# The output gate as a fifth seven-product pair, with the heads' steps reordered

## The chip, the cores and the metric

The kernel runs on one core of one Trainium2 chip. The metric is the device time in microseconds (us). The core has a matrix engine, TensorE (PE), whose weight loads the profile shows apart (PEld); a vector engine (DVE); a scalar engine (ACT); GpSimd (POOL); and SyncE (SP), which issues most of the transfers. Each engine works through its own instructions in order; semaphores tie them together.

## The reference

One layer of an encoder for 256 tokens of width 2048, in float32. The parts are a SwiGLU feed-forward part (width 5632) with a layer norm, a mixer with a layer norm, a second SwiGLU part with a layer norm, and a gated embedding at the end. The change touches the mixer alone, which computes:

```python
proj = x @ w_in
mq, mk, mv, mo, mi, mf, sq, sk, sv, ga, gb = _split_cols(proj)
qk = silu(_causal_conv(concatenate([mq, mk]), conv_w))
h = _mlstm_chunkwise(q_m, k_m * 256 ** -0.5, mv, log_i, log_f)      # 4 heads of 256
h = _head_norm(h, norm_g)
y_m = h * sigmoid(mo)                                               # mo: the output gate, 1024 columns
y_sb = _stick_breaking(sq, sk, sv)                                  # 8 heads of 128
merged = sigmoid(ga) * (y_m @ w_up_m) + sigmoid(gb) * (y_sb @ w_up_sb)
return merged @ w_out
```

## The kernel before, in words

The tokens stand in two halves of 128 (index `t`). Every large product is a list of **units**. A unit takes 256 rows of a weight (one tile of 128 x 2 x up to 512 columns) and one half of the tokens. Both operands are split into a high and a low float32r part, so that a unit is two k-halves of three matmuls (lines 1210 to 1215). A weight tile is loaded by a transfer on SP's queue (`loads`, line 1128). It is then split: ACT copies out the high part (line 1162), DVE subtracts to give the low one (line 1166). `limits` (line 1116) says how many raw tiles may be loaded ahead and how many splits may stand ready. In the mixer these two numbers are `room`, set on the way by `rooms(...)` entries in the program.

**Seven products for eight.** `seven` (line 321) multiplies the two token halves by two weight blocks with Strassen's scheme: 7 products instead of 8, from sums of weight blocks and from sums of activations (`act.forms`, made by `form_turn`, line 286). The sums of weights are made partly by accumulating transfers on POOL's queue (`grow`, line 337), partly on DVE (`plus`, line 342). The results gather in four PSUM banks named X, E, B, W; B and W are two banks kept for it (`seeded`). `done(m, banks)` is called as each product ends. `chained` (line 374) strings several such pairs together, so that the first product of the next pair runs within the present one, and puts in empty places (`None`) where a sum has to land first. `weave` (line 157) spreads this side list evenly over a main list.

**The order of work.** The Python program itself fixes the order of instructions on every engine. It walks the list of units and keeps a clock of its own, `sched.now`, that each unit pushes on (line 1216). Small steps (transposes, heads, activations) are generators in a heap. Each `yield DELAY[...]` sets a step due so many microseconds later on that clock, and due steps are written out between two units. `wait(...)` asks again every 0.6 us whether a flag is set; `sched.until` runs steps early if a unit needs them. A delay that is too short lets an in-order engine stand before work that is not ready.

**The mixer.** After the first query columns and the gates' columns (line 924) the main list runs: key columns of heads 0 and 1, value columns, output-gate columns `mo`, then queries, keys, values and `mo` of heads 2 and 3, then the six column groups of the stick-breaking heads, then the products with `w_up_m` (`ups(g, 0)`). The side list woven in is the four pairs of merge gates (`gates7`). `mo_done` (line 784) takes each group of `mo` out of PSUM by a sigmoid on ACT and multiplies it with the norm's weights on POOL. `conv` (line 745) transposes and convolves queries and keys. `mlstm(h)` (line 813) is one head: decay matrix (line 817), scores (828), values (840), norm, gate (861), transposes (866). The heads run two in sequence, `mlstm(0)` and `mlstm(1)`, later `mlstm(2)` and `mlstm(3)`. Their outputs are kept in DRAM for a while: `away` (line 798) stores them, `back` (line 804) loads them shortly before they are needed, both on POOL's queue. `stick(h)` (line 875) is one stick-breaking head, two chains of four; it has two masks on POOL (lines 891 and 900) and ends in the matmul of line 906.

All tiles of 4 KB per partition (raw, split, activations, gates) come from one pool of 44 pages; a new tile waits until the last user of its page is done.

Of the kernel before, what the change touches and what calls it, by code (L numbers as in the profile page):

```python
# [8 lines left out]
F32 = mybir.dt.float32  # L9
# [4 lines left out]
P = 128  # L14
# [31 lines left out]
    "sbt": 6.0, "g0": 3.0, "g1": 4.0, "g2": 12.0, "cv0": 1.0, "cv1": 6.0, "turn": 3.5, "apart": 9.0, "copied": 2.5, "away": 6.0, "refill": 14.0, "cv2": 1.3,  # L46
    "m0": 3.0, "m1": 0.6, "m2": 1.2, "m3": 4.6, "m4": 4.6, "s0": 6.6, "s1": 6.7, "s2": 4.0,
# [133 lines left out]
def kernel(  # L181
# [563 lines left out]
    def conv(which, g, stage):  # L745
        yield from wait("cw")
        for e in range(2):
# [8 lines left out]
            acc = temp().rearrange("q (k s) -> q k s", s=S)  # L756
            for k in range(2):
                b = 8 * which + 2 * h + k
                w = lambda j: st["cw"][:, j * 16 + b:j * 16 + b + 1]
                activate(acc[:, k], ps[:, k], ACT.Copy, scale=w(3))  # L760
                for j in range(3):
                    d = 3 - j
                    nc.vector.scalar_tensor_tensor(out=acc[:, k, d:], in0=ps[:, k, :S - d], scalar=w(j),
                                                   in1=acc[:, k, d:], op0=ALU.mult, op1=ALU.add)
# [19 lines left out]
    def mo_done(g):  # L784
        def done(ps, t):
            if ("mo", t) not in st:
                st["mo", t] = big()
            cs = slice(g * COL, (g + 1) * COL)
            activate(st["mo", t][:, cs], ps, ACT.Sigmoid)
            nc.gpsimd.tensor_tensor(out=st["mo", t][:, cs], in0=st["mo", t][:, cs],  # L790
                                    in1=st["nm"][:, cs], op=ALU.mult)
# [21 lines left out]
    def mlstm(h):  # L813
        yield from wait("gates", ("qk", 0, h), ("qk", 1, h), ("v", 0, h // 2), ("v", 1, h // 2))
# [41 lines left out]
        yield from wait(("mo", 0, h // 2), ("mo", 1, h // 2))  # L856
# [396 lines left out]
```

## Time and profile before

| | us |
|---|---|
| median of 3 runs | 2198.45 |
| the three runs | 2197.73, 2198.45, 6001.9 |
| profiled execution | 2197.17 |
| its span, first to last instruction | 2195.5 |
| PE busy | 2175.7 (99%) |
| DVE busy | 1789.3 (82%) |
| ACT busy | 1333.5 (61%) |
| POOL busy | 241.2 (11%) |

The third run took 6001.9 us; the other two lie within 0.03% of each other. A row of a group of instructions in the profile reads: line, engine, operation, what it writes <- what it reads, shapes, count | busy us, mean ns of one | idle time of the engine just before them, and what ended it. A row of waits reads: who <- for whom: us in total, times, longest. A row of a timeline reads: start, duration, engine, line, operation. L with a number is a line of the kernel.

### The profile page before, as it was taken

The numbers are of one execution on the slowest core, as the hardware profiler recorded it, in microseconds if no ns is written. First come the engines' busy times: TensorE is split into PE (matmuls) and PEld (weight loads), VectorE is DVE, ScalarE is ACT, GpSimd is POOL, SyncE is SP. The second block draws the span as 40 slices with busy tenths as digits, with TensorE's granted clock in tenths as the row PEclk, the third lists the DMA queues.
The fourth block names the chain that finished last, engine by engine and source line by source line (L and its number), as shares of the span: only waits on it lengthen the run. The fifth ranks groups of instructions, "written<-read, shape, count | busy, mean of one in ns | idle before, by whom it ended". The sixth has DMA issues, their size and how long they took to land.

```text
span 2195.5 us, 27768 instructions
## 1 busy us (share of the span) xinstructions
PE 2175.7 (99%) x9972; PEld 1801.3 (82%) x9972; DVE 1789.3 (82%) x1967; ACT 1333.5 (61%) x1600; POOL 241.2 (11%) x209
## 2 busy tenths in 40 slices
PE   9999999999999999999999999999999999999999
PEld 7888888888887888888887888888888888888878
DVE  6889988888898778877676777599898989889884
ACT  6556565666575666766575644556666666666562
POOL 3111101111100001011022100011011101110000
PEclk9999999999999999999999999999999999999999
DMA  9899889887993858879678876679878998899652
GB/s 347 221 256 268 254 240 301 270 245 208 292 328 115 255 140 255 225 225 270 206 196 252 261 265 200 213 161 316 262 228 243 305 259 248 241 278 300 214 167 72
DMA packets 274346, 527.06 MB, mean 240 GB/s; under 512 B 16640, under 2 KB 25760, under 8 KB 273952
## 3 DMA queue, kind: packets, MB, share of 16 engines
q1 hardware_dynamic: 229248, 435.10, 58.5%
q0 software_dynamic: 44960, 90.19, 22.4%
q8 instruction: 78, 1.28, 0.2%
q14 instruction: 60, 0.49, 0.1%
HBM read 518.93 MB, written 6.29 MB: 239 GB/s over the span
## 4 chain that ended last, share of the span: by engine, by line
PE 94%; DVE 2%; ACT 2%; issue 1%; DMA 1%; POOL 0%; DVEq 0%; ACTq 0%
PE mm L1214 26%; PE mm L1215 25%; PE mm L1213 25%; PE seeded L1214 5%; PE seeded L1215 5%; PE seeded L1213 5%; PE ms L267 1%; DVE split L1166 1%; ACT split L1162 1%; DMA aside<-actT 1%; ACT temp L239 0%; PE ms L456 0%; POOL temp L891 0%; PE ms L906 0%; PE ms L840 0%
## 5 line engine op out<-in xcount | busy, mean ns | idle before, releaser
L1166 DVE TENSOR_TENSOR split<-raw,split 128x1024 fp32r<-128x1024 f32 (+2 forms) x1061 | 1241.6, 1205 | 221.5 <-ACT split L1162 209.5
L1162 ACT CAST split<-raw 128x1024 fp32r<-128x1024 f32 (+2 forms) x1061 | 1066.8, 1038 | 443.0 <-PE mm L1214 119.1
L1213 PE MATMUL mm<-split,actT 128*128 128x512 f32 (+2 forms) x2640 | 1026.7, 389 | 2.8 <-ACT big L1069 2.3
L1214 PE MATMUL mm<-split,actT 128*128 128x512 f32 (+2 forms) x2640 | 1015.3, 385 | 4.7 <-DVE split L1166 4.7
L1215 PE MATMUL mm<-split,actT 128*128 128x512 f32 (+2 forms) x2640 | 1015.3, 385 | 2.3 <-DVE actT L272 2.3
L1214 PEld LDWEIGHTS mm<-split,actT 128*128 128x128 f32 x2640 | 496.4, 188 | 103.0 <-DVE split L1166 8.3
L1215 PEld LDWEIGHTS mm<-split,actT 128*128 128x128 f32 x2640 | 495.9, 188 | 102.1 <-DVE actT L272 3.1
L1213 PEld LDWEIGHTS mm<-split,actT 128*128 128x128 f32 x2640 | 496.2, 188 | 99.7 <-ACT big L1069 3.2
L337 POOL DMA_DIRECT2D raw<-in_ffn_w_dram x128 | 153.9, 1216 | 1159.8 <-DVE split L1166 961.9
L342 DVE TENSOR_TENSOR raw<-raw 128x1024 f32<-128x1024 f32 x160 | 195.3, 1221 | 12.8 <-DMA raw<-in_ffn_w_dram 10.6
L1214 PE MATMUL seeded<-split,actT 128*128 128x512 f32 x480 | 187.1, 390 | 1.8 <-DVE split L1166 1.8
L1213 PE MATMUL seeded<-split,actT 128*128 128x512 f32 x480 | 188.6, 393 | 0.0
L1215 PE MATMUL seeded<-split,actT 128*128 128x512 f32 x480 | 187.0, 390 | 0.0
L571 DVE SCALAR_TENSOR_TENSOR xres<-mm,xres 128x512 f32<-128x512 f32 x160 | 109.1, 686 | 21.9 <-PE mm L1215 21.9
L1214 PEld LDWEIGHTS seeded<-split,actT 128*128 128x128 f32 x480 | 90.2, 188 | 20.6 <-DVE split L1166 2.5
L1215 PEld LDWEIGHTS seeded<-split,actT 128*128 128x128 f32 x480 | 90.1, 188 | 18.8
L1213 PEld LDWEIGHTS seeded<-split,actT 128*128 128x128 f32 x480 | 90.2, 188 | 18.0
L269 ACT CAST actT<-ms 128x512 fp32r<-128x512 f32 x60 | 35.2, 587 | 85.2 <-PE ms L267 85.1
L337 POOL DMA_DIRECT2D raw<-in_w_in_dram x32 | 38.5, 1208 | 269.8 <-DVE split L1166 262.8
L272 DVE TENSOR_TENSOR actT<-ms,actT 128x512 fp32r<-128x512 f32 x60 | 41.1, 686 | 25.0 <-ACT actT L269 15.2
L239 ACT ACTIVATE temp<-mm 128x512 f32<-128x512 f32 (+1 forms) x38 | 21.8, 574 | 57.8 <-PE mm L1215 57.8
L235 ACT ACT_TABLE_LOAD x36 | 46.2, 1283 | 0.6
(154 smaller groups left out, 724.5 us busy)
## 6 DMA issues: line engine op xcount, KB each, us to landing
raw<-in_ffn_w_dram SPq DMA_DIRECT2D x527, 512.0 KB, 8.0
raw<-in_w_in_dram SPq DMA_DIRECT2D x168, 512.0 KB, 5.0
raw<-in_ffn_w_dram POOLq DMA_DIRECT2D x128, 512.0 KB, 9.4
raw<-in_w_in_dram POOLq DMA_DIRECT2D x32, 512.0 KB, 8.1
raw<-in_w_out_dram SPq DMA_DIRECT2D x32, 512.0 KB, 4.9
raw<-in_w_ple_gate_dram SPq DMA_DIRECT2D x24, 512.0 KB, 5.4
raw<-in_w_up_m_dram SPq DMA_DIRECT2D x16, 512.0 KB, 5.3
raw<-in_w_up_sb_dram SPq DMA_DIRECT2D x16, 512.0 KB, 5.2
```

What stands on the lines that cost most here:

```text
L235: nc.scalar.preload_act_table_set(table[0])
L267: nc.tensor.transpose(ps[:, k], src[:, k * P:(k + 1) * P], ident[:])
L269: nc.scalar.copy(dst[:, 0], ps[:])
L272: nc.vector.tensor_tensor(out=dst[:, 1], in0=ps[:], in1=dst[:, 0], op=ALU.subtract)
L337: nc.gpsimd.dma_start(out=raw.tile[:, :, :cols], in_=src.src, accum_op=ALU.add)
L342: nc.vector.tensor_tensor(out=a.tile[:, :, :cols], in0=a.tile[:, :, :cols], in1=b.tile[:, :, :cols], op=ALU.add)
L571: nc.vector.scalar_tensor_tensor(out=xs, in0=ps, scalar=0.5, in1=xs, op0=ALU.mult, op1=ALU.add)
L1162: nc.scalar.copy(hi[:, ks], r[:, ks])
L1166: nc.vector.tensor_tensor(out=lo[:, ks], in0=r[:, ks], in1=hi[:, ks], op=ALU.subtract)
L1213: nc.tensor.matmul(ps, hi, w[0][:, k, :u.cols], start=first, stop=False, skip_group_check=u.onto)
L1214: nc.tensor.matmul(ps, hi, w[1][:, k, :u.cols], start=False, stop=False, skip_group_check=u.onto)
L1215: nc.tensor.matmul(ps, lo, w[0][:, k, :u.cols], start=False, stop=last, skip_group_check=u.onto)
```

## The change

The output gate leaves the main list. Its two groups of 512 columns become the two weight blocks of one more seven-product pair, put ahead of the four pairs of merge gates in the side list. The code of `gates7` becomes `sigmoid7`, which both use. A sigmoid's result is then multiplied with the norm's weights on DVE, 2.5 us later on the program's clock, and not on POOL. A head now waits for its half of the output gate before its first step and no longer before its last ones; head 2 waits 9 more. Three delays grow (cv0, m1, s2). In `conv` both ACT copies come before the DVE sums. Some `rooms` are smaller, and one stands earlier. `back` comes eight entries before the end of the column groups instead of four, and loads on SP's queue instead of POOL's; the stored tiles are float32 on both sides.

```diff
-    "sbt": 6.0, "g0": 3.0, "g1": 4.0, "g2": 12.0, "cv0": 1.0, "cv1": 6.0, ...
-    "m0": 3.0, "m1": 0.6, "m2": 1.2, "m3": 4.6, "m4": 4.6, "s0": 6.6, "s1": 6.7, "s2": 4.0,
+    "sbt": 6.0, "g0": 3.0, "g1": 4.0, "g2": 12.0, "cv0": 2.5, "cv1": 6.0, ...
+    "m0": 3.0, "m1": 2.5, "m2": 1.2, "m3": 4.6, "m4": 4.6, "s0": 6.6, "s1": 6.7, "s2": 5.5,
...
+            w = lambda k, j: st["cw"][:, j * 16 + 8 * which + 2 * h + k:j * 16 + 8 * which + 2 * h + k + 1]
             for k in range(2):
-                b = 8 * which + 2 * h + k
-                w = lambda j: st["cw"][:, j * 16 + b:j * 16 + b + 1]
-                activate(acc[:, k], ps[:, k], ACT.Copy, scale=w(3))
+                activate(acc[:, k], ps[:, k], ACT.Copy, scale=w(k, 3))
+            for k in range(2):
                 for j in range(3):
...
-    def mo_done(g):
-        def done(ps, t):
...
-            activate(st["mo", t][:, cs], ps, ACT.Sigmoid)
-            nc.gpsimd.tensor_tensor(out=st["mo", t][:, cs], in0=st["mo", t][:, cs],
-                                    in1=st["nm"][:, cs], op=ALU.mult)
-            flags.add(("mo", t, g))
-        return done
+    def mo_place(t, g):
+        if ("mo", t) not in st:
+            st["mo", t] = big()
+        return st["mo", t][:, g * COL:(g + 1) * COL]
+
+    def mo_after(t, g):
+        c = mo_place(t, g)
+        sched.spawn(mo_scaled(t, g, c), DELAY["copied"])
+
+    def mo_scaled(t, g, c):
+        nc.vector.tensor_tensor(out=c, in0=c, in1=st["nm"][:, g * COL:(g + 1) * COL], op=ALU.mult)
+        flags.add(("mo", t, g))
...
-    aside = {(c, t): dram_pool.tile([P, 2, 4, P], F32R, name=f"aside{c}{t}") for c in range(2) for t in range(TT)}
+    aside = {(c, t): dram_pool.tile([P, 2, 4, P], F32, name=f"aside{c}{t}") for c in range(2) for t in range(TT)}
...
-        nc.gpsimd.dma_start(out=aside[c, t][:], in_=ymT.tiles[c, t][:])
+        nc.gpsimd.dma_start(out=aside[c, t][:], in_=ymT.tiles[c, t][:].bitcast(F32))
...
-                nc.gpsimd.dma_start(out=ymT.tiles[c, t][:], in_=aside[c, t][:])
+                nc.sync.dma_start(out=ymT.tiles[c, t][:].bitcast(F32), in_=aside[c, t][:])
...
     def mlstm(h):
-        yield from wait("gates", ("qk", 0, h), ("qk", 1, h), ("v", 0, h // 2), ("v", 1, h // 2))
+        yield from wait("gates", ("qk", 0, h), ("qk", 1, h), ("v", 0, h // 2), ("v", 1, h // 2),
+                        ("mo", 0, h // 2), ("mo", 1, h // 2))
+        if h == 2:
+            yield DELAY["apart"]
...
-        yield from wait(("mo", 0, h // 2), ("mo", 1, h // 2))
...
-            main += [rooms(9)] + columns(COL, COL, qk_done(0, 1)) + [rooms(9)] + columns(1024 + COL, COL, qk_done(1, 1))
+            main += [rooms(9)] + columns(COL, COL, qk_done(0, 1)) + [rooms(8)] + columns(1024 + COL, COL, qk_done(1, 1))
...
-        main += columns(3072 + g * COL, COL, mo_done(g))
...
-            main.append(rooms(12 if first == 2 else 10))
+            main.insert(len(main) - (0 if first == 2 else 6), rooms(11 if first == 2 else 7))
...
-    def gates7(g):
+    def sigmoid7(wa, wb, col0, place, after):
...
-        def gate(t, half, src, sign):
+        def part(t, half, src, sign):
             activate(place(t, half), src, ACT.Sigmoid, scale=sign)
-            flags.add(("gate", g, half, t))
+            after(t, half)
...
+        return seven(wa, wb, D, col0, COL, x1T, done)
...
-    main.insert(len(main) - 4, back)
+    main[len(main) - 8:len(main) - 8] = [back]
...
-    program.extend(weave(main, chained([gates7(g) for g in range(4)])))
+    program.extend(weave(main, chained([sigmoid7(w_in[:, 3072:], w_in[:, 3072 + COL:], 0, mo_place, mo_after)] + [gates7(g) for g in range(4)])))
```

More of the change, by code (lines that the diff above doesn't have):

```diff
@@ L782, in load_norm_m @@
         nc.sync.dma_start(out=st["nm"][:], in_=norm_m[0].partition_broadcast(P))
[L784 to L793 removed]
+    def mo_place(t, g):
[8 more added lines that the diff above has]
+        flags.add(("mo", t, g))
+        return
+        yield
     ymT, ysbT = ActT(act_tile), ActT(act_tile)
[L796 removed]
+    aside = {(c, t): dram_pool.tile([P, 2, 4, P], F32, name=f"aside{c}{t}") for c in range(2) for t in range(TT)}
     def away(c, t):
[L799 removed]
+        nc.gpsimd.dma_start(out=aside[c, t][:], in_=ymT.tiles[c, t][:].bitcast(F32))
         pages[0] -= 1
@@ L946 @@
     gt = {}
-    def gates7(g):
-        def place(t, half):
-            if (g, t) not in gt:
-                assert g > 1 or "spilt" in flags
-                gt[g, t] = xres[t][:, g * 1024:(g + 1) * 1024] if g < 2 else big()[:]
-            return gt[g, t][:, half * COL:(half + 1) * COL]
+    def sigmoid7(wa, wb, col0, place, after):
         def done(m, banks):
@@ L968, in done @@
             elif m == 2:
-                sched.spawn(gate(0, 0, ps["X"], 1.0), DELAY["silu"])
+                sched.spawn(part(0, 0, ps["X"], 1.0), DELAY["silu"])
             elif m == 7:
```

19 lines of the change are left out of this document (13 added, 6 removed).

## The prediction

> **What bounds the kernel now.** I read the page from the top: the span, the busy shares, the chain that ended last.
>
> ```profile
> span 2195.5 us, 27768 instructions
> PE 2175.7 (99%) x9972; PEld 1801.3 (82%) x9972; DVE 1789.3 (82%) x1967; ACT 1333.5 (61%) x1600; POOL 241.2 (11%) x209
> PE 94%; DVE 2%; ACT 2%; issue 1%; DMA 1%; POOL 0%; DVEq 0%; ACTq 0%
> ```
>
> TensorE (PE) is idle for 2195.5 − 2175.7 = 19.8 us in the whole run, and 94% of the chain lies on it. The page counts pipelined matmuls as busy, so I check at what pace they come, in the timeline of PE at a place without a gap:
>
> ```profile
> 902.54 0.39 PE L1213 MATMUL mm<-split,actT 128*128 128x512 f32 x1
> ...
> 907.98 0.39 PE L1213 MATMUL mm<-split,actT 128*128 128x512 f32 x1
> ```
>
> Between these rows lie 24 matmuls of 512 columns: 5.44 us, 0.227 us from start to start, although each row lasts 0.39. One work unit of the program (two k-halves of three matmuls) is thus 1.36 us. The time can fall in two ways: fewer matmuls, or less idle PE.
>
> The edits lie in the mixer. I compare windows: mixer, and the second FFN, in which seven-product pairs are woven in more densely.
>
> ```profile
> core 0: us, PE busy (x) PEld busy (x) DVE busy (x) ACT busy (x) POOL busy (x), PEclk, DMA share, GB/s
> 715.00:1260.00 545.00, 539.81 (x2523) 446.37 (x2522) 404.25 (x500) 351.60 (x461) 71.62 (x64) 1.00 0.80 229
> 1420.00:2080.00 660.00, 659.47 (x2955) 545.50 (x2955) 589.89 (x607) 403.56 (x436) 77.24 (x64) 1.00 0.88 257
> ```
>
> In the mixer PE idles 545.00 − 539.81 = 5.19 us at full clock; in the FFN only 0.53 us, with VectorE (DVE) 89% busy against 74% here. So a denser DVE does not by itself cost PE time. The waits of PE in the mixer's window:
>
> ```profile
> PE seeded L1214 <- DVE split L1166: 1.8, 2, 1.2
> PE ms L677 <- DVE big L683: 1.4, 1, 1.4
> PE ms L906 <- POOL temp L900: 0.9, 1, 0.9
> PE mm L1214 <- DVE split L1166: 0.8, 2, 0.7
> PE ms L840 <- DVE temp L830: 0.2, 1, 0.2
> ```
>
> Five causes, 5.1 us together (total, times, longest). That is all that reordering alone can win in this stage.
>
> **The change part by part.** *The matmuls.* Two groups of 512 output-gate columns now take 2 x 8 row pairs x 2 token halves = 32 units. As a seven-product pair they take 7 products x 4 = 28. Four units less is 24 matmuls, on the engine that sets the end: −5.44 us, the very stretch quoted above. The shape, the operands and the banks (mm and seeded) are those of the four pairs already there, so I see no reason for another pace. The Trainium skill (TensorE: Matmul & The Clock Gate, Back-to-back issue gap) gives a sustained spacing of about 131 ns for 512 columns; by it the estimate would be 24 x 0.131 = 3.1 us. The trace disagrees, with 227 ns over 24 matmuls, and decides.
>
> *What the other engines get.* Sixteen weight tiles, each used twice, become 28, each used once: 12 more splits. Besides come 8 sums on DVE (line 342), 8 accumulating loads on GpSimd's (POOL's) queue (line 337), and the copies and differences of the bank work. The products with the norm (line 790) go from POOL to DVE.
>
> ```profile
> L1166 DVE TENSOR_TENSOR split<-raw,split 128x1024 fp32r<-128x1024 f32 x230 | 274.1, 1224 | 94.6 <-ACT split L1162 93.7 <-PE mm L1214 0.2
> L1162 ACT CAST split<-raw 128x1024 fp32r<-128x1024 f32 x230 | 231.6, 1049 | 44.1 <-PE mm L1214 13.5 <-DMA aside<-actT 8.4 <-PE seeded L1214 6.4
> L342 DVE TENSOR_TENSOR raw<-raw 128x1024 f32<-128x1024 f32 x32 | 39.2, 1224 | 2.2 <-DMA raw<-in_w_in_dram 2.2
> L337 POOL DMA_DIRECT2D raw<-in_w_in_dram x32 | 38.5, 1208 | 269.8 <-DVE split L1166 262.8 <-DVE hrs L857 7.0
> L962 DVE TENSOR_TENSOR seeded<-mm,temp 128x512 f32<-128x512 f32 x4 | 2.8, 697 | 2.1 <-ACT temp L960 2.1
> L960 ACT COPY temp<-mm 128x512 f32<-128x512 f32 x4 | 2.3, 585 | 3.4 <-PE mm L1215 3.4
> L790 POOL TENSOR_TENSOR big<-big 128x512 f32<-128x512 f32 x4 | 5.5, 1386 | 35.2 <-ACT big L239 35.1
> L235 ACT ACT_TABLE_LOAD x26 | 33.4, 1283 | 0.5
> ```
>
> DVE: 12 x 1.224 + 8 x 1.224 + about 6 x 0.697 (two in the bank work, four products) = 28.7 us, so 433 us of some 540, 80%. ScalarE (ACT): 12 x 1.049 + 3 x 0.585 = 14.3 us, so 68%; the sigmoids at other times may bring or spare some table loads of 1.283. POOL: 8 x 1.208 − 5.5 = +4.2 us. I cost all of it at nothing: its cover is the splits that stand ready (up to four in the mixer), and the FFN window carries 89% DVE under an idle PE of 0.53 us. Where the cover is gone, a late split costs up to 1.2 us (row of waits).
>
> *Order in time.* Weaving 163 side entries over 200 main units instead of 132 over 232 raises the density from 0.57 to 0.82. To place events I count units of 1.36 us from the start of the weave:
>
> ```profile
> L695 ACT COPY gst<-mm x2: 166/177/188, 743.3 to 743.7; 128x8 f32<-128x8 f32 x2
> 798.95 0.69 PE L817 MATMUL ms<-big 4*128 4x256 f32 x2
> 841.01 0.69 PE L817 MATMUL ms<-big 4*128 4x256 f32 x2
> ```
>
> It starts near 743. The gate's last product is side entry 43, behind 53 main and 32 side units: 743 + 85 x 1.36 = 859, with transposes between some 864. A head waits for it at its front now, so heads 0 and 1 start near 865 and not at 799. A head takes 841.01 − 798.95 = 42.1 us, 44 with the longer m1: the pair runs to 953. The second value columns are done after 131 units, near 935, so head 2 (9 later) overlaps head 1 by some 10 us. This wait is one of the program's writer, not of an engine: nothing is queued behind it. The rest of the stage needs the heads only in the ups, by the same count some 200 us on. The overlap can cost a late split, 0 to 1.2 us twice; I take +0.6.
>
> *Delays.* m1 from 0.6 to 2.5 covers the 0.2 us at line 840. The conv's two ACT copies now stand ahead of its six DVE sums; what it saves, the ACT's idle time between, isn't on PE's path: nothing. cv0 only moves transposes. s2 from 4.0 to 5.5 and the move of `back` act on the 0.9 us at line 906. Its cause:
>
> ```profile
> 1185.80 5.87 POOL L891 TENSOR_SCALAR_AFFINE_SELECT temp<-temp 128x256 f32<-128x256 f32 x1 [3.57 <-DVE temp L890]
> 1191.63 0.40 POOL L900 TENSOR_SCALAR_AFFINE_SELECT temp<-temp 128x256 f32<-128x256 f32 x1
> 1185.64 1.22 DVE L342 TENSOR_TENSOR raw<-raw 128x1024 f32<-128x1024 f32 x1
> 1186.78 4.63 DVE L1166 TENSOR_TENSOR split<-raw,split 128x1024 fp32r<-128x1024 f32 x4
> ```
>
> A mask of 0.4 us took 5.87, and the next one, for which PE waited, stood behind it. 1.5 us more covers 0.9: −0.9 us.
>
> *`back` on SP.* Four loads leave POOL's queue for SP's and come four entries of the main list sooner. On SP the weight loads stand behind them, and ACT's splits wait for those. The nearest rows:
>
> ```profile
> ACT split L1162 <- DMA aside<-actT: 8.4, 2, 7.2
> raw<-in_w_in_dram SPq DMA_DIRECT2D x168, 512.0 KB, 5.0
> actT<-aside POOLq DMA_DIRECT2D x4, 512.0 KB, 8.1
> ```
>
> ACT once stood 7.2 us for a page that an outgoing store still held, and PE lost under 0.8 us by it (the row of waits at mm L1214). Nor does ACT's row of splits name a weight load among its three largest waits, so the smaller rooms (8, 11 and 7 tiles ahead) have slack. Bounds: 0 to 7.2 us; I take 0, near to what PE lost. The ups have no wait for these loads now, so sooner wins nothing.
>
> *Sum.* −5.44 + 0.6 − 0.2 − 0.9 = −5.9 us. The profiled execution took 2197.17 us (span 2195.5), so 2191.2. The timed runs lie higher: 2197.73 and 2198.45 are 0.9 above it on average, and the third, 6001.9, says nothing of the kernel. Forecast: 2192.1 us.
>
> **The rivals.** *All of the mixer's idle time goes* (17%): the delays and rooms act on each of the five causes, so 2198.1 − 5.44 − 5.19 = 2187.4. Against it: 2.6 us of the five are late splits, and splits come more often now.
>
> *The masks hold PE up* (8%, slower than before). Each of eight sticks has a mask just ahead of its last matmul (line 906). If each costs PE the 0.9 us of the one row, that is 6.3 more than now: 2198.1 − 5.44 + 6.3 = 2199.0; at 1.4, the longest wait of the stage, 2203. It decides from the seventh such wait on. For it: the mask of 5.87 us beside five DVE instructions, of which there will be more. Against it: one wait in eight now, and 1.5 us more room. The Trainium skill (SBUF — State Buffer, Who interferes with whom) says that "A DVE instruction with two SBUF inputs contends with a GpSimd instruction that reads SBUF" and that the later one blocks until the first ends; the mask above, which ended 0.26 us after the five, agrees, and by that rule the 24 such instructions added make this rival likelier.
>
> *The loads run dry* (9%): `back` or a store holds SP or a page while few tiles stand ahead, and the 7.2 us of ACT reach PE: 2198.1 − 5.44 + 7.2 = 2199.9, from one occurrence on. Against it: it happened once, and the splits in hand took it.
>
> That the change doesn't do what it says can be left out: 28 units stand in the code.
>
> **How the numbers follow.** The forecast has 62%; its own range, with splits' waits between none and four more of 1.2, is 2189 to 2196. Four per cent remain for what no row shows. The range of 2187 to 2199 takes in the forecast and most of the first rival, and reaches to the lower edge of the other two. Left out are some 5% below 2187, the upper halves of the two slower rivals (9%) and the remainder (4%). Two per cent, about what a measurement of this kernel can tell from no change, are 44 us. Faster by that would need more than all idle PE time (19.8) and the matmuls together: 1%. Slower needs 50 us of new waits, where the longest of PE in the mixer is 1.4, or a second run like 6001.9: 3%. Within: 96%.
>
> **What would show it.** PE's matmuls in the mixer's window fall by 24 at the same 0.227 us. The wait at line 906 is gone, POOL's products too; splits grow by 12, sums by 8. Heads start near 865. PE's waits in the mixer sum to 3 to 7 us. I am wrong if they pass 10, if the masks lead them, if ACT waits for weight loads, or if idle time appears outside the mixer.

## The result and the profile after

The changed kernel took 2218.92 us (median of four runs, 2216.64 to 2221.86), the kernel before 2198.09 (median of the three runs already shown and one more, 2196.72). It is slower by 1%, or 20.8 us, where 6 us less was forecast. The ratio on record, 1.0099 with a 95% interval of 1.0086 to 1.0112, leaves the run of 6001.9 us out, which the medians do not; 20.8 us lies within its interval.

The profiled execution was the slowest of the four, 2221.86 us. The head of its page, the line of the engines and that of the chain's shares:

```profile
span 2220.1 us, 27824 instructions
PE 2182.7 (98%) x9948; PEld 1801.6 (81%) x9948; DVE 1812.8 (82%) x1993; ACT 1348.9 (61%) x1617; POOL 248.2 (11%) x209
PE 85%; DVE 4%; issue 4%; DMA 4%; ACT 3%; POOL 1%; SPq 0%; DVEq 0%; POOLq 0%; ACTq 0%
```

The 24 matmuls are gone (9972 to 9948), yet PE is *busy* 7 us longer, and idle for 37.4 us instead of 19.8. Both belong to the loss: more waiting, and stretches in which matmuls are slower. The windows say where. Columns: window, its length, then busy us and count of PE, PEld, DVE, ACT and POOL, the granted clock of PE (1.00 is full speed), DMA share, GB/s. The first two rows answer to those shown of before:

```profile
715.00:1260.00 545.00, 522.86 (x2398) 427.46 (x2397) 407.28 (x506) 354.18 (x464) 78.15 (x64) 0.98 0.80 226
1420.00:2080.00 660.00, 658.52 (x2952) 544.86 (x2951) 586.66 (x598) 415.42 (x456) 77.30 (x64) 1.00 0.89 259
870.00:930.00 60.00, 50.01 (x208) 39.79 (x208) 43.09 (x64) 35.61 (x46) 4.44 (x4) 0.89 0.50 136
913.00:922.30 9.30, 9.07 (x21) 6.44 (x22) 3.20 (x5) 5.12 (x7) 0.41 (x1) 0.50 0.31 81
```

The mixer's window holds 2398 of PE's instructions, before 2523. Twenty-four no longer exist, so the program is 101 behind at 1260 us, at 0.227 us each 22.9 us: nearly all of the 24.6 by which the span grew. The FFN's window is as full as it was (2952 to 2955). The worst 60 us of the mixer are 870 to 930: 208 instructions at a mean clock of 0.89. Before it held:

```profile
870.00:930.00 60.00, 58.77 (x269) 48.28 (x268) 47.91 (x59) 41.84 (x53) 6.02 (x6) 1.00 0.85 236
```

DVE and ACT did not take PE's place there: they too are less busy than before. The engines stood for each other. PE's waits in the mixer after the change (who <- for whom: us, times, longest; lines 1213 to 1215 are now 1223 to 1225, the split's 1166 is 1176, the product with the values, 840, is 847, the head's transposes 866 are 872):

```profile
PE mm L1224 <- DVE split L1176: 7.3, 8, 1.8
PE ms L872 <- DVE temp L763: 6.9, 1, 6.9
PE ms L847 <- DVE temp L837: 3.3, 1, 3.3
PE mm L1223 <- ACT temp L671: 1.8, 1, 1.8
PE seeded L1224 <- DVE split L1176: 1.5, 4, 0.6
PE ms L901 <- POOL temp L897: 0.2, 1, 0.2
```

With one of 0.5 and one of 0.4 that are left out here they sum to 21.9 us, where before had 5.1. The longest, 6.9 us, is one event. PE's timeline around it (start, duration, line; in brackets the idle time and what ended it):

```profile
895.71 0.39 PE L1225 MATMUL seeded<-split,actT 128*128 128x512 f32 x1
...
900.70 0.39 PE L1223 MATMUL mm<-split,actT 128*128 128x512 f32 x1
902.84 0.50 PE L1224 MATMUL mm<-split,actT 128*128 128x512 f32 x1 [1.76 <-DVE split L1176]
...
905.51 0.60 PE L752 MATMUL ms<-ident,temp 128*128 128x128 f32 x4
905.95 0.38 PE L872 MATMUL ms<-ident,temp 128*128 128x128 f32 x2
913.23 0.66 PE L872 MATMUL ms<-ident,temp 128*128 128x128 f32 x2 [6.90 <-DVE temp L763]
...
918.12 0.63 PE L1224 MATMUL mm<-split,actT 128*128 128x512 f32 x1
...
922.39 0.44 PE L1225 MATMUL mm<-split,actT 128*128 128x512 f32 x1
```

Up to 900.70 the pace is the old one (22 matmuls in 4.99 us, 0.227 each). Then PE transposes a block of keys for the convolution (L752), and at once, with no unit between, head 0's output (L872). The first half of the head's transposes goes through, the second waits until the convolution's sums have been read out of PSUM by DVE. What DVE had ahead of that:

```profile
905.61 1.22 DVE L1176 TENSOR_TENSOR split<-raw,split 128x1024 fp32r<-128x1024 f32 x1
906.75 1.22 DVE L342 TENSOR_TENSOR raw<-raw 128x1024 f32<-128x1024 f32 x1
907.88 2.35 DVE L1176 TENSOR_TENSOR split<-raw,split 128x1024 fp32r<-128x1024 f32 x2
910.15 2.93 DVE L763 SCALAR_TENSOR_TENSOR temp<-ms,cw,temp 128x253 f32<-128x253 f32 x6
```

Between the transposes at 905.5 and the sums at 910.15 stand splits and weight sums: DVE's in-order queue is some 5 us long. The head's own input was ready (its last product, L867, began at 905.27), so what is missing is a PSUM bank; by the code, the two accumulators, X, E, the convolution's block and the head's first half hold all that are left beside B and W. Afterwards the clock is at half for 9.3 us (the row 913.00:922.30): from 918.12 to 922.39 ten matmuls start, one every 0.427 us. The clock had fallen inside the wait: the trace's granted clock changes to a half at 908.82, 2.5 us after the wait began, and back to full at 922.48. Nothing in the prediction had allowed for it. The Trainium skill (TensorE: Matmul & The Clock Gate, What's actually happening, and Wait — 56ns, not 53.3ns?) has the array at half clock after an idle window of about 3.4 us, and a start-to-start of 426.7 ns for 512 columns while cold. The spacing agrees; the idle time does not, for here 2.5 us were enough.

ACT, before, named no weight load among the main causes of its waits. Now:

```profile
ACT split L1172 <- DVE raw L342: 20.3, 12, 3.3
ACT split L1172 <- DMA raw<-in_w_in_dram: 14.4, 5, 6.3
```

One of these, at 966 us, stands ahead of the 3.3 us of line 847. ACT's timeline there:

```profile
966.00 1.05 ACT L1172 CAST split<-raw 128x1024 fp32r<-128x1024 f32 x1 [6.26 <-DMA raw<-in_w_in_dram]
967.07 1.28 ACT L235 ACT_TABLE_LOAD   x1
968.36 0.73 ACT L239 ACTIVATE temp<-ms,aT 128x256 f32<-128x256 f32 x2
```

ACT stands 6.26 us in front of a split whose tile is not there; a head's exponentials (L239, behind a table load) come after it in ACT's order, and the step on PE which needs them is late. Another 2.08 us on the way go to DVE, which waits for the load of a sum until 970.38, and 3.4 to that sum and two splits in front of the head's step.

### The profile page after: what moved, and what is told of

Same layout as the page of the kernel before. It is cut to its first block, busy times and chain, and to the rows that moved or that the text cites. A ratio compares the mean times of both kernels' runs of the same rounds, so it can differ in the third digit from the quotient of the medians.

```text
span 2220.1 us, 27824 instructions
## 1 busy us (share of the span) xinstructions
PE 2182.7 (98%) x9948; PEld 1801.6 (81%) x9948; DVE 1812.8 (82%) x1993; ACT 1348.9 (61%) x1617; POOL 248.2 (11%) x209
## 4 chain that ended last, share of the span: by engine, by line
PE 85%; DVE 4%; issue 4%; DMA 4%; ACT 3%; POOL 1%; SPq 0%; DVEq 0%; POOLq 0%; ACTq 0%
PE mm L1224 23%; PE mm L1225 23%; PE mm L1223 23%; PE seeded L1225 4%; PE seeded L1223 4%; PE seeded L1224 4%; DVE split L1176 2%; DMA raw<-in_ffn_w_dram 2%; ACT split L1172 1%; DMA raw<-in_w_in_dram 1%; PE ms L267 1%; ACT temp L239 1%; DMA aside<-actT 0%; DVE temp L763 0%; PE ms L456 0%
## 5 line engine op out<-in xcount | busy, mean ns | idle before, releaser
L1176 DVE TENSOR_TENSOR split<-raw,split 128x1024 fp32r<-128x1024 f32 (+2 forms) x1073 | 1256.8, 1206 | 214.1 <-ACT split L1172 195.5
L1172 ACT CAST split<-raw 128x1024 fp32r<-128x1024 f32 (+2 forms) x1073 | 1079.6, 1038 | 474.9 <-PE mm L1224 120.2
L1224 PE MATMUL mm<-split,actT 128*128 128x512 f32 (+2 forms) x2608 | 1006.9, 386 | 11.4 <-DVE split L1176 11.3
L1224 PEld LDWEIGHTS mm<-split,actT 128*128 128x128 f32 x2608 | 491.9, 189 | 111.5 <-DVE split L1176 18.1
L342 DVE TENSOR_TENSOR raw<-raw 128x1024 f32<-128x1024 f32 x168 | 204.8, 1219 | 20.2 <-DMA raw<-in_ffn_w_dram 10.4
L1224 PE MATMUL seeded<-split,actT 128*128 128x512 f32 x504 | 197.7, 392 | 1.5 <-DVE split L1176 1.5
L1223 PE MATMUL seeded<-split,actT 128*128 128x512 f32 x504 | 199.1, 395 | 0.0
L1225 PE MATMUL seeded<-split,actT 128*128 128x512 f32 x504 | 197.0, 391 | 0.0
L571 DVE SCALAR_TENSOR_TENSOR xres<-mm,xres 128x512 f32<-128x512 f32 x160 | 109.0, 686 | 21.9 <-PE mm L1225 21.9
L1224 PEld LDWEIGHTS seeded<-split,actT 128*128 128x128 f32 x504 | 95.0, 188 | 22.7 <-DVE split L1176 3.7
L1225 PEld LDWEIGHTS seeded<-split,actT 128*128 128x128 f32 x504 | 95.0, 188 | 19.7
L1223 PEld LDWEIGHTS seeded<-split,actT 128*128 128x128 f32 x504 | 95.2, 189 | 19.4 <-issue 0.3
L337 POOL DMA_DIRECT2D raw<-in_w_in_dram x40 | 48.4, 1215 | 299.3 <-DVE split L1176 216.8
L239 ACT ACTIVATE temp<-mm 128x512 f32<-128x512 f32 (+1 forms) x38 | 21.8, 574 | 58.0 <-PE mm L1225 57.9
```

What stands on the lines that cost most here:

```text
L239: nc.scalar.activation(out, in_, func, **kw)
L337: nc.gpsimd.dma_start(out=raw.tile[:, :, :cols], in_=src.src, accum_op=ALU.add)
L342: nc.vector.tensor_tensor(out=a.tile[:, :, :cols], in0=a.tile[:, :, :cols], in1=b.tile[:, :, :cols], op=ALU.add)
L571: nc.vector.scalar_tensor_tensor(out=xs, in0=ps, scalar=0.5, in1=xs, op0=ALU.mult, op1=ALU.add)
L1172: nc.scalar.copy(hi[:, ks], r[:, ks])
L1176: nc.vector.tensor_tensor(out=lo[:, ks], in0=r[:, ks], in1=hi[:, ks], op=ALU.subtract)
```

## The experiments

Two families of causes were at stake: places (a step that stands badly, a wait that can be moved) and work (more on DVE and in the loads than the mixer can hide). For all of them the table gives the time over the kernel before of the same set of runs (2196.7 to 2197.1 us), and the ratio with its interval; the changed kernel, timed in the first set alone, is 20.8 over. An interval reaches some 1.5 parts in a thousand to each side, about 3 us: smaller differences between two rows are not clear of noise.

| label | us | over before | ratio |
|---|---|---|---|
| pair_alone | 2227.10 | +30.0 | 1.0137 [1.0121, 1.0152] |
| heads_early | 2210.54 | +13.5 | 1.0062 [1.0047, 1.0077] |
| rooms_as_before | 2215.24 | +18.2 | 1.0085 [1.0070, 1.0100] |
| head0_turns_late | 2208.76 | +11.7 | 1.0052 [1.0035, 1.0068] |
| rooms_and_late | 2205.88 | +9.1 | 1.0038 [1.0024, 1.0051] |
| patient | 2206.26 | +9.5 | 1.0043 [1.0027, 1.0060] |
| patient_rooms | 2208.73 | +11.9 | 1.0055 [1.0037, 1.0073] |
| patient_rooms_loads | 2212.29 | +15.5 | 1.0071 [1.0053, 1.0089] |
| splits_five | 2204.91 | +8.2 | 1.0038 [1.0025, 1.0051] |
| splits_six | 2223.00 | +26.1 | 1.0120 [1.0105, 1.0135] |
| raws_more | 2222.20 | +25.5 | 1.0115 [1.0099, 1.0130] |
| sums_ahead | 2210.68 | +14.0 | 1.0061 [1.0046, 1.0076] |
| sums_by_load | 2210.47 | +13.6 | 1.0061 [1.0044, 1.0078] |
| sums_by_load_2 | 2208.44 | +11.7 | 1.0053 [1.0038, 1.0068] |
| all_sums_by_load | 2231.59 | +34.8 | 1.0158 [1.0143, 1.0174] |
| before_more_dve | 2207.93 | +11.1 | 1.0049 [1.0034, 1.0064] |
| before_denser | 2217.99 | +21.3 | 1.0098 [1.0083, 1.0113] |
| pause | 2217.00 | +20.1 | 1.0091 [1.0076, 1.0106] |

Five of them came out above every range that was given for them: `splits_six`, `raws_more`, `all_sums_by_load`, `before_denser` and `patient_rooms`. `heads_early` and `head0_turns_late` lie between the ranges of the two theories.

### The parts of the change

**pair_alone**: the kernel before with the fifth pair and nothing else of the change (the product with the norm on POOL, heads, delays, rooms and `back` as before).

```diff
-        main += columns(3072 + g * COL, COL, mo_done(g))
...
-    program.extend(weave(main, chained([gates7(g) for g in range(4)])))
+    program.extend(weave(main, chained([sigmoid7(w_in[:, 3072:], w_in[:, 3072 + COL:], 0, mo_place, mo_after)] + [gates7(g) for g in range(4)])))
```

> The kernel before with the seven-product pair for the output gate alone: the heads wait for the gate late as before, conv order, delays, rooms and the way back are those of before, the product with the norm stays on POOL. Theory collision (the heads, moved onto the convolutions by their wait at the front, fill VectorE and PSUM; PE waits and its clock then drops): head 0 starts near 800 but is held at its late wait until the gate is done near 864, so part of the collision stays; 2195 to 2208. Theory work (the pair's own splits, sums and loads are too much for the mixer): 2212 or more. Theory rooms (fewer tiles ahead leave ACT waiting for weight loads): 2192 to 2195, no wait of PE over 2 us.

The pair alone costs 30.0 us; the other edits win 9 of it back. PE's waits in its mixer:

```profile
PE mm L1215 <- DMA actT<-aside: 6.4, 1, 6.4
PE mm L1216 <- DVE split L1168: 5.6, 8, 1.8
PE ms L864 <- DVE temp L762: 4.6, 1, 4.6
PE ms L904 <- POOL temp L898: 1.7, 1, 1.7
```

The heads' outputs come back too late by 6.4 us; a mask (L898) holds PE 1.7 us; the changed kernel, with the moved `back` and the longer s2, has neither wait. The head's transposes wait behind the convolution here too (4.6). So the small edits together do their work, though no run takes one of these two out by itself. What they mend is made by the pair.

**heads_early**: the changed kernel, with the heads' wait for the output gate back before the norm, and no 9 us more for head 2.

```diff
-        yield from wait("gates", ("qk", 0, h), ("qk", 1, h), ("v", 0, h // 2), ("v", 1, h // 2),
-                        ("mo", 0, h // 2), ("mo", 1, h // 2))
-        if h == 2:
-            yield DELAY["apart"]
+        yield from wait("gates", ("qk", 0, h), ("qk", 1, h), ("v", 0, h // 2), ("v", 1, h // 2))
...
+        yield from wait(("mo", 0, h // 2), ("mo", 1, h // 2))
```

> The changed kernel, but the heads wait for the output gate only before their norm, as before, and head 2 isn't held back by 9. Theory collision: heads 0 and 1 no longer stand at the same program point as the convolutions' second half; the wait of 6.9 us at the head's transposes and the slow clock behind it go, some 12 to 15 us: 2204 to 2207. Theory work and theory rooms: the heads' place matters little, 2214 or more.

**head0_turns_late**: the changed kernel, with head 0's transposes 9 us later and no other edit.

```diff
-        yield DELAY["m4"]
+        yield DELAY["m4"] + (9.0 if h == 0 else 0.0)
```

> The changed kernel with one delay more: head 0's transposes come 9 us later, seven units behind the convolution's transposes and not right after them. Theory collision: the 6.9 us at the head's transposes was a wait for a PSUM bank that the convolution still held; it goes, with the slow clock behind it: 2204 to 2208. Theories work and rooms: VectorE's backlog is there all the same, PE waits elsewhere for late splits, 2214 or more.

Both take the head off the convolution, and both win: 20.8 over before becomes 13.5 and 11.7. The second is the sharper test, for it moves only head 0's transposes and what follows them in the heads' own order. The line of 6.9 us is gone; late splits remain (11.0 us in 15 waits).

**rooms_as_before**: the changed kernel with the old `rooms`.

```diff
-            main += [rooms(9)] + columns(COL, COL, qk_done(0, 1)) + [rooms(8)] + ...
+            main += [rooms(9)] + columns(COL, COL, qk_done(0, 1)) + [rooms(9)] + ...
...
-            main.insert(len(main) - (0 if first == 2 else 6), rooms(11 if first == 2 else 7))
+            main.append(rooms(12 if first == 2 else 10))
```

> The changed kernel with the rooms of before (9, 12 and 10 tiles ahead instead of 8, 11 and 7). Theory rooms: ACT's waits for weight loads (14.4 us in the mixer) go, and with them the wait of 3.3 us at the values' product and the slow clock behind it: 2208 to 2211, and 2195 if this is all of it. Theory collision: the wait of 6.9 us stays; 2210 to 2219. Theory work: no change, 2216 to 2222.

It wins 2.6 us, less than the intervals can tell by themselves. ACT's waits for weight loads fall from 14.4 to 4.0 us, but PE's 6.9 and the wait at line 847 (3.1) stay. The place of ACT's long wait shows why:

```profile
961.70 1.05 ACT L1172 CAST split<-raw 128x1024 fp32r<-128x1024 f32 x1 [5.42 <-DMA aside<-actT]
```

In front of the same table load and exponentials ACT now stands 5.42 us for a page that the outgoing store of a head still holds. The cause changed, the wait stayed.

**rooms_and_late**: both edits together.

> The changed kernel with head 0's transposes 9 us later and the rooms of before. If the two causes are separate, their gains add: 2218.9 - 10.1 - 3.7 = 2205. If both are one and the same backlog, less than half of the second is left: 2207 to 2209.

9.1 us over before: the two gains add (20.8 − 9.1 − 2.6), and the rooms bring the same 2.6 a second time. PE's waits are then almost of one kind:

```profile
PE mm L1224 <- DVE split L1176: 8.3, 10, 1.8
PE seeded L1224 <- DVE split L1176: 0.8, 1, 0.8
```

With the 5.4 us that the pair saves, some 14.5 us are still lost; in the profiled execution, a faster one of 2204.03 us, 12.2. Waits are only a part of these: PE is idle for 27.4 us (before: 19.8), 7.6 more, and busy for 2174.9, which is 4.6 more than 2175.7 less the 5.4. The clock is full throughout there. Matmuls behind a wait come slower for a while even so (in the changed kernel, after the 1.76 us at 902.84, ten starts take 2.44 us, 0.244 each); no run takes the two parts apart. The rest of the runs asked what the loss is for.

### Is it DVE's added work?

**before_more_dve**: the kernel before, with 24 more operations on DVE where the output gate's weights pass, 29 us of work, and nothing else. Like the sums, they stand between a tile's load and ACT's copy of it (ACT waits 6.6 us for them). They take the maximum of a raw weight tile with itself, in place, so nothing changes in the result.

```diff
+    def extra(raw, n):
+        def make():
+            for _ in range(n):
+                nc.vector.tensor_tensor(out=raw.tile[:], in0=raw.tile[:], in1=raw.tile[:], op=ALU.max)
+        return make
...
-        main += columns(3072 + g * COL, COL, mo_done(g))
+        mo = columns(3072 + g * COL, COL, mo_done(g))
+        for k, u in enumerate(mo[::2]):
+            u.tile.make = extra(u.tile.raw, 1 + k % 2)
+        main += mo
```

> The kernel before with 24 more VectorE instructions of the sums' size at the output gate's weight tiles (each writes the larger of a tile and itself, so nothing is changed by it): 29 us more of VectorE work in the mixer, about what the pair brings, without any other edit. Theory work: 2205 or more. Theory collision: 2197 to 2200, since heads, convolutions and gate stand apart there.

It costs 11.1 us. First the windows' row of its mixer, then PE's waits there:

```profile
715.00:1260.00 545.00, 533.03 (x2477) 439.67 (x2476) 420.21 (x513) 346.06 (x456) 73.00 (x64) 0.99 0.79 225
```

```profile
PE mm L1223 <- DVE split L1175: 2.8, 3, 1.2
PE ms L846 <- DVE temp L836: 2.7, 1, 2.7
PE seeded L1223 <- DVE split L1175: 1.8, 2, 1.2
```

DVE is at 77% (420.21 of 545), far from full. PE's waits rise from 5.1 to 12.0 us: those for splits on DVE from 2.6 to 4.6, all others from 2.5 to 7.4. The longest is at a head's product with the values, which comes before its input is ready now that DVE has more in front of it. The shape of the loss is that of `rooms_and_late`: PE is idle 6.8 us more and busy 3.9 more. This is the run that decides on the term that the prediction put at nothing.

**sums_by_load**, **sums_by_load_2**: `head0_turns_late`, with the new pair's sums of weights made by accumulating loads and not on DVE (8 sums of 1.22 us). In the first a quarter of the output gate is taken before its last product is in, so there its share is missing; the second takes it behind that product.

```diff
-        return seven(wa, wb, D, col0, COL, x1T, done)
+        return seven(wa, wb, D, col0, COL, x1T, done, grown)
...
-    ... 0, mo_place, mo_after)] + [gates7(g) for g in range(4)])))
+    ... 0, mo_place, mo_after, True)] + [gates7(g) for g in range(4)])))
```

> The changed kernel with head 0's transposes 9 us later and, besides, the gate pair's 8 sums on VectorE replaced by accumulating transfers (the scheme's other form, with its third product before the seventh). Theory sums (ACT and so the splits wait behind the pair's sums on VectorE, 22 us of ACT's idle time): half of the waits before 990 us go, 2202 to 2205. Theory elsewhere: 2207 to 2211, or more if the transfers come late.

> As sums_by_load, but the second half's sigmoid of the gate is taken as the seventh product ends and no longer as the third does (there it came a product too early, so that part of the output gate was wrong, and PE waited 6.8 us for it). Theory sums (VectorE's extra work makes splits late): that wait goes and the waits for splits stay low, 2202 to 2204. Theory elsewhere: 2207 to 2211.

No gain (+11.7 both with and without). PE's late splits fall from 11.0 to 6.0 us, but a new wait of 2.6 at a high part comes, and ACT's waits for weight loads rise from 11.3 to 21.0.

**all_sums_by_load**: `rooms_and_late`, with all five pairs' sums made by loads.

> The changed kernel with head 0's transposes 9 us later, the rooms of before, and in all five pairs the sums made by accumulating transfers, none by VectorE: some 49 us less VectorE work in the mixer, 20 transfers more. Theory work (about 0.37 us of time for each us of VectorE work, as before_more_dve showed): 10 us or more below rooms_and_late, 2190 to 2197. Theory transfers: they come late, and what VectorE gives PE loses again, 2200 to 2212.

34.8 us over before. The windows' row of its mixer, then its ACT's main wait there:

```profile
715.00:1260.00 545.00, 520.18 (x2382) 422.37 (x2380) 363.34 (x462) 353.73 (x462) 115.39 (x103) 0.99 0.93 242
```

```profile
ACT split L1175 <- DMA raw<-in_w_in_dram: 44.6, 15, 7.9
```

Over the whole run DVE is busy 41 us less than in `rooms_and_late` (1771.0 for 1812.3). But in the mixer the DMA engines are 93% busy (82% there), and what ACT waits for most is weight loads. Less work on DVE is no help if the transfers pay for it.

### Is it the chain from load to sum to split?

ACT's largest wait in the changed kernel is for sums on DVE (20.3 us). **sums_ahead**: `rooms_and_late`, with each sum in the mixer written one split earlier.

```diff
+                if limits(j) is room:
+                    make(j + 3)
```

> rooms_and_late (2205.9 us as measured) with the sums on VectorE written out one split earlier in the mixer. ACT's 20 us of waiting for sums (14 times) is the mark of a chain: the sum stands behind a subtraction on VectorE, ACT's copy waits for the sum, the next subtraction waits for ACT. Theory chain: with the sum one place ahead ACT's waits fall to 8 us and PE's waits for splits from 8 to 4 us; 2199 to 2202. Theories four splits, loads and density: 2204 to 2208; more if the sums now wait for loads.

**splits_five**, **splits_six**: up to five (six) splits ready instead of four; the first on `rooms_and_late`, the second on `head0_turns_late`.

```diff
-    main = [rooms(13, 4)] + columns(1024, COL, qk_done(1, 0)) + [rooms(8)]
+    main = [rooms(13, 5)] + columns(1024, COL, qk_done(1, 0)) + [rooms(8)]
```

> rooms_and_late with five splits in hand in the mixer instead of four. Theory four splits: PE's waits for splits halve and its waits at the heads' steps, which stand behind more splits, grow less than that; 2200 to 2204. If the lesson of splits_six holds (what the splits gain, the steps of heads and convolutions lose): 2205 to 2212.

> The changed kernel with head 0's transposes 9 us later (2208.8 us as measured) and, besides, six splits in hand in the mixer instead of four. Theory late splits (what is left of the loss, some 13 us against the sum of the prediction, is PE waiting for splits that VectorE finishes late, because each split is now used up in one unit more often than in two): with 7 to 8 us of splits in hand instead of 5 to 6 the waits for splits fall from 11 us to 3; 2198 to 2202. Theory backlog (VectorE itself is too full there): the same waits come later, 2206 to 2210.

**raws_more**: `rooms_and_late` with one or two raw tiles more throughout (14, 10, 11, 11, 14, 12, 12 for 13, 8, 9, 9, 12, 10, 10).

> rooms_and_late with two more raw tiles ahead everywhere in the weave (10, 11, 14 and 12). Theory loads: 2201 to 2203. Else 2204 to 2208, since ACT waits for no weight load there any more.

Each does what it says and none wins. With `sums_ahead` ACT no longer waits for sums, but DVE waits longer for the sums' loads (14.7 us for 6.1), and the time rises by 4.9. With five splits PE's waits for splits fall from 9.1 to some 3 us and those at steps rise by about as much: the time is the same. With six it is 14.4 us worse than its base; of its PE waits:

```profile
PE ms L824 <- DVE actT L262: 5.8, 2, 5.1
PE ms L847 <- DVE temp L837: 5.2, 4, 1.7
PE ms L752 <- ACT temp L740: 4.6, 2, 2.9
PE mm L1224 <- DVE split L1176: 2.5, 3, 1.5
```

The splits are in time now, the steps are late: a split made ahead stands in DVE's and ACT's queues in front of a step that is due. More raw tiles take pages from the 44: ACT's longest waits are then for a page's last readers, DVE (31.1 us) and PE (28.5 us; 13.6 and 15.3 in `rooms_and_late`), and the time rises by 16.4.

### Is it the delays?

**patient**: `head0_turns_late` with longer delays for every step of heads, convolutions and sticks. **patient_rooms**: the same with the old rooms. **patient_rooms_loads**: that with the new pair's sums by loads.

```diff
-    "sbt": 6.0, ... "cv0": 2.5, ...
-    "m0": 3.0, "m1": 2.5, "m2": 1.2, "m3": 4.6, "m4": 4.6, "s0": 6.6, "s1": 6.7, "s2": 5.5,
+    "sbt": 8.0, ... "cv0": 4.5, ...
+    "m0": 5.0, "m1": 4.5, "m2": 1.2, "m3": 7.0, "m4": 8.0, "s0": 8.0, "s1": 8.0, "s2": 7.0,
```

> The changed kernel with head 0's transposes 9 us later and longer delays between the steps of heads, sticks and convolutions (m0 5, m1 4.5, m3 7, m4 8, sbt 8, s0 8, s1 8, s2 7, cv0 4.5); nobody needs these steps early. Theory steps too tight (a fuller VectorE finishes the steps' work later than their delays allow): PE's waits at steps go, but they are only some 5 us of the 16 left: 2203 to 2206. Theory late splits: the splits' waits of 11 us stay, 2206 to 2210.

> Head 0's transposes 9 later, the rooms as before the change, and every step of heads, conv and sticks due 0.8 to 3.4 us later. If the three gains add (2218.9 - 10.2 - 3.7 - 2.5), 2202.5: steps' waits gone, ACT without a wait for weight loads, late splits of 6 to 9 us left. If what is taken from one wait only appears in another: 2205 to 2207, the splits' waits at 9 or more.

> As patient_rooms, and the new pair's sums of weights made by accumulating loads instead of by DVE (8 sums of 1.22 us, 10 us of DVE's work). If DVE's work in the mixer is what makes splits late, their waits fall from some 8 to 4 us and the time to 2198 to 2200. If the loads only take over (as they did with the smaller rooms): the same within 2 us of patient_rooms, with ACT's waits for weight loads back.

With the changed kernel's rooms the longer delays win 2.2 us and the waits at steps go. With the old rooms they lose 2.8 against `rooms_and_late`, though each edit alone was a gain; the intervals overlap in both comparisons. PE's waits for splits are 10.0 us there, those at steps below 2. The sums by loads cost 3.6 more, as ACT's waits for weight loads come back (12.8 us). From here on the gains of single edits no longer add.

### Is it the order alone?

**before_denser**: the kernel before, same work, only that its four pairs are woven over the first 162 main units instead of all; density 0.81, about that of the changed kernel.

```diff
-    program.extend(weave(main, chained([gates7(g) for g in range(4)])))
+    cut = [i for i, u in enumerate(main) if isinstance(u, Unit)][162]
+    program.extend(weave(main[:cut], chained([gates7(g) for g in range(4)])) + main[cut:])
```

> The kernel before with its four pairs woven over the first 162 units of the main list and not over all 232: the density of side entries is 0.81 as in the changed kernel, without any added work. Theory density: waits for splits of 5 to 8 us more, 2201 to 2206. Else 2196 to 2199.

It costs 21.3 us without a single added operation. Its PE waits, in the mixer up to 1300 us, since the stage ends later here:

```profile
PE ms L906 <- POOL temp L900: 4.9, 2, 3.2
PE ms L866 <- DVE actT L262: 4.5, 1, 4.5
PE mm L1215 <- DVE split L1167: 4.1, 5, 1.3
PE ms L895 <- POOL temp L891: 2.3, 1, 2.3
PE ms L752 <- ACT temp L740: 1.4, 1, 1.4
```

The most, 7.2 us, goes to masks of the last sticks (lines 906 and 895). From 1256.35 to 1270.16 PE runs only small matmuls of these sticks, for the next products need their output and no unit stands between, and the clock is at half from 1263.59 to 1273.83. The changed kernel has no such end. Again a head's transposes wait once for long (4.5). Late splits, which the expectation was about, grow little (4.4 us with the `seeded` ones, before 2.6). Delays and rooms of this kernel fit one order of the work; another order pays for that, whether it brings work or not. It isn't the same order as the changed kernel's (here the pairs end early, and no side entries are left for the sticks), so this can't be set against the 14.5 us one to one.

### What does a pause cost beyond itself?

**pause**: the kernel before, with one transpose on PE, after the mixer, that waits for eight operations on POOL.

```diff
...
+        for _ in range(8):
+            nc.gpsimd.tensor_scalar(out=t[:], in0=t[:], scalar1=ALPHA, scalar2=None, op0=ALU.mult)
+        ps = misc([P, P])
+        nc.tensor.transpose(ps[:], t[:, 0:P], ident[:])
...
```

> The kernel before with one pause of PE in the stage of the output weights: one transpose waits for eight GpSimd instructions of about 1.56 us on a tile that nothing else uses, 6 to 10 us of idle PE. Theory clock: behind the pause some 30 matmuls run at half the pace (0.43 us instead of 0.227), so the time grows by the wait plus 5 to 7 us. Theory no clock: it grows by the wait alone, as if the slow stretch in the changed kernel were the backlog's.

```profile
PE ms L1034 <- POOL temp L1032: 16.6, 1, 16.6
```

The span of the profiled execution grew by 18.1 us for a wait of 16.6. The windows' row behind the pause reads:

```profile
1344.30:1348.30 4.00, 4.00 (x12) 3.13 (x12) 0.00 (x0) 0.00 (x0) 0.00 (x0) 0.56 0.00 0
```

Behind the wait half clock lasts 4 us and costs some 1.8 (nine starts of matmuls take 3.86 us; at 0.227 they would take 2.04), less than the expectation had. In the changed kernel the slow stretch behind the shorter wait of 6.9 us lasted 9.3 us. The trace's granted clock says more, if one reads when it changes. It is at half throughout these two windows, of the changed kernel and of `pause`:

```profile
908.90:922.40 13.50, 9.17 (x22) 6.45 (x23) 7.16 (x12) 5.22 (x7) 0.41 (x1) 0.50 0.22 59
1330.80:1347.80 17.00, 3.77 (x10) 3.00 (x11) 8.65 (x6) 2.09 (x2) 12.59 (x8) 0.50 0.31 94
```

The first stretch lasts from 908.82 to 922.48, the second from 1330.78 to 1347.85: 13.65 and 17.07 us, four and five times 3.41. Leaving out the first and last 15 us of each trace, the 20 traces have 33 stretches of half clock, and all are one to five times 3.41 us long. So what a wait costs beyond itself depends on more than its length: the same wait of 6.9 us in `rooms_as_before` began a stretch of 10.24. Why the step from 915.65 to 919.06 in the changed kernel, full of work on PE, did not bring the clock back isn't settled; a head's small matmul (line 824) lies in it.

## Why the prediction was wrong

**The matmuls: right.** 24 fewer, pace 0.227 where nothing waits. The 24 matmuls, 5.44 us at this pace, are gone from the trace; the saving is only smaller than what came with it. Two of the prediction's own signs of being wrong came: waits in the mixer over 10 us (21.9), and ACT waiting for weight loads (14.4).

**"I cost all of it at nothing": the first wrong step.** The counts were right (splits 1061 to 1073 in the whole run, sums 160 to 168), but the cover was chosen by busy share. The FFN window at 89% DVE is another case: 496 of its 590 us are splits and sums, and the program lets five splits and 16 raw tiles stand ready there, against four and 7 to 13 in the mixer. In the mixer DVE, at 74%, also has steps on which PE waits directly, and these stand in order behind the splits. 29 us of work put into the kernel before cost 11.1 us (`before_more_dve`), at 77%. The stated bound, "a late split costs up to 1.2 us", was also low: a late split cost up to 1.8 in the changed kernel, and a late step 2.7 in `before_more_dve` and 3.3 at line 847.

**"The overlap can cost a late split ... I take +0.6": the second.** Head 0 did start where the count put it (line 824 at 869.4; 865 was forecast). The overlap that was priced never came: head 1 ended at 951.5, and head 2 began at 961.3, not near 944. I looked at the overlap of heads with each other and not at what else lies at the heads' new place. Head 0's transposes fell on a block of the convolution of later keys; together they lacked a PSUM bank. `head0_turns_late` shows 9.1 us for it, of which 6.9 are the wait; that the rest is the half clock is read from the trace, not tested by itself.

**"The smaller rooms (8, 11 and 7 tiles ahead) have slack": wrong by some 2.6 us** (`rooms_as_before`). The rival *the loads run dry* had the mechanism, and its price of 7.2 was too high: with the smaller rooms ACT stood 6.26 us for a load, with the old ones 5.42 for a page that a store held, and PE waited 3.3 and 3.1 behind it.

**`back` on SP and the delays: half right.** On SP the loads harmed nothing visible, so 0 of 0 to 7.2 us was right. "Sooner wins nothing" was not: with the pair, the old place and the old queue PE waits 6.4 us for them (`pair_alone`). The wait for the mask at line 906 (now 912) is gone as forecast; 0.2 us are left at the other mask's (901). So the rival *the masks hold PE up* is refuted for this kernel; `pair_alone`, with the old s2, has 1.7 us of it. The 0.2 us at line 840 became 3.3 at 847 instead of going.

**The sum.** 20.8 + 5.4 = 26.2 us of losses against 0.6 forecast: 9.1 at head 0, 2.6 at the rooms, 14.5 left. The range took the rivals one by one, each with one price, and ended at 2199. It had no case in which several come together, and none in which PE's clock falls.

**What stays open.** The 14.5 us. That DVE's added work makes most of it is likely by size (11.1 us in the kernel before). It isn't shown, since a part of that work (8 sums, 10 us) given to transfers brought no gain (`sums_by_load_2`, `patient_rooms_loads`), and the order alone can cost as much (`before_denser`, though with a loss at the end of the sticks that the changed kernel doesn't have). ACT's added work (15 us by the two pages, also put at nothing) was not tested by itself. Splits, sums, raw tiles, loads and delays were each moved once; each time waits came up at another engine or step, or the time stayed where it was within the intervals. No version here beats the kernel before; the best is 8.2 us slower.

## What to carry to other kernels

Price work added to an engine that is off the critical path by who stands behind it in that engine's order and waits for it, not by the engine's busy share. Before steps move in time, list what already lies at their new place and count the PSUM banks that both hold. A saving of 24 matmuls (5.4 us) is less than one wait of 7 us, even without the slow clock behind it. So in a kernel whose order is fitted by hand, expect to fit delays and buffer limits anew before such a saving can be seen.

## What was not expected of the hardware

A single wait of 6.9 us on PE was followed by 9.3 us at a granted clock of 0.50, with matmuls every 0.427 us instead of 0.227; the wait of 3.3 us at line 847 was followed by 6.1 us of it. The wait of 16.6 us in `pause` was followed by only 4. The length of the slow stretch doesn't follow the length of the wait: half clock comes in whole steps of 3.41 us (from one to five in these traces), and all but three of the stretches begin within a wait of over 1 us or less than 1.5 us behind it. Nor is a long wait needed: in `before_more_dve` a stretch of 3.41 us began at 801.05, 0.3 us behind a wait of 1.21.
